# Encoder layer on one core: closer dense jobs beside attention, and partial results added before they are weighed

## The chip, the cores and the metric

The kernel runs on one core of a Trainium2 chip. The metric is the device time of one execution in microseconds (us), the median of several runs. The engines are TensorE (PE, matmuls, with PEld for its weight loads), VectorE (DVE), ScalarE (ACT), GpSimd (POOL) and SyncE (SP), which issues most of the transfers.

## The reference

One layer of an encoder, with a width of 1024, 2048 rows and one sequence:

```python
mod = c_act @ w_ada[l] + b_ada[l]
h = rmsnorm(x, g_norm1[l]) * (1.0 + sc1) + sh1
proj = h @ w_in[l]
q_sb, k_sb, v_sb, q_ca, k_ca, v_ca = jnp.split(proj, split_pts, axis=-1)
o_sb = stick_breaking_attention(...)        # 8 heads of 64, causal
o_ca = chunked_relpos_attention(...)        # 8 heads of 64, own chunk and 8 before it
mixed = jnp.concatenate([o_sb, o_ca], axis=-1)
x = x + gt1 * (mixed @ w_o[l])
h = rmsnorm(x, g_norm2[l]) * (1.0 + sc2) + sh2
x = x + gt2 * (jnp.square(jax.nn.relu(h @ w1[l])) @ w2[l])   # 1024 -> 4096 -> 1024
```

All of it is float32. The stick-breaking heads weigh a key by its own sigmoid and by the product of one minus the sigmoids of the keys between.

## The kernel before

Every float32 operand is split into a high part (rounded to the matmul's fp32r) and a low part (the rest), and a product takes three matmuls: high by high, high by low, low by high. ACT copies the high part, DVE (or POOL) subtracts it. Rows are worked on in four blocks of 512.

The stages follow each other: projections (0 to 413 us of the span), attention (413 to 1290), a seam, and the MLP (1330 to the end). PE, DVE, ACT and POOL run their instructions in the order in which the program issues them.

**Attention** is a list of units: one head `h`, one block of rows `g` and, for the stick-breaking heads, one block of keys. Each has four steps. In a step, PE computes scores (`z`), ACT and DVE turn them into weights (DVE's scan is `p`), PE transposes the weights of a unit eight steps older (`wt`), ACT and DVE split them (`wth`, `wtl`), and PE multiplies them with the values (`acc`). The softmax heads' names begin with `c`. Blocks of rows are taken in the order 2 and 3 together, 1, 0.

PE has time left in a step, which is filled with dense matmuls of 512 columns. They come from jobs that are run one after the other: the projections of the row blocks 1 and 0 (`fill_qkv`, banks `pf`), and the output projection of the blocks 2, 3 and 1 (`outproj`, banks `po`, eight banks of 24 matmuls). Each job is a generator: it yields a number for a matmul, a function for work that is put off, and the words "ahead" and "wait". `fill`, called once in a step, adds the step's share to a credit and takes matmuls from the job while the credit is at least one. At "wait", which each job yields once before its first matmul, it sets a rest from `RESTS`: for so many steps no dense matmul is taken. At "ahead", which a job yields near its end, the next job's `ahead` issues transfers: input tiles (`fx`) and one set of weights (`ow` or `fw`). The tiles come in groups of four from rotating pools, so a group's transfer has to wait until the tiles that it overwrites have been used.

When both heads of a pair are done, `finish` adds their halves on POOL, and some steps later `keep` splits the result (ACT copies `os`, POOL subtracts) and stores it. `values` in `fill_qkv` does the same split for the value projections, with ACT and DVE.

**The MLP** saves matmuls with sums and differences of operand blocks: a group takes seven products instead of eight. Five groups of its second matmul, class `Outer` with `i` in (7, 2, 5, 3, 4), run the products 1, 5, 6, 3, 7, 2, 4 in this order. A product has eight steps of six matmuls. For each step ACT and DVE make the operands (`opr`, `ol`), eight steps ahead, and DVE also makes sums of the right-hand operand (`r`, `half_sum`). At a product's end its two banks (`ps`, `ps_s`) go to the output blocks that they belong to: `weigh` on DVE multiplies a bank by the gate and adds it to an output tile `x`. In the groups 7 and 5, the blocks "22" and "12" each take two products and go into two output tiles per half. The output tiles are loaded with the residual by `load_x`.

Of the kernel before, what the change touches and what calls it, by code (L numbers as in the profile page):

```python
# [9 lines left out]
F32 = mybir.dt.float32  # L10
# [3 lines left out]
ALU = mybir.AluOpType  # L14
# [65 lines left out]
def encoder_kernel(ctx, tc, xT, c, g1, g2, w_in, w_rest, gqk, bias, w_o, w1, w2, w_ada, b_ada, out):  # L80
# [602 lines left out]
    if True:  # L683
# [36 lines left out]
        def finish(u):  # L720
            r = (u.h % 2) * HD
            q = HD - r
            if u.h % 2 == 0:
                pend["o", u.g] = op.tile([P, TB], F32, tag="o", name=f"o{u.nm}")
            o = pend["o", u.g]
            tmp = op.tile([P, TB], F32, tag="otmp", name=f"otmp{u.nm}")
            rows = slice(r, r + HD)
            act.copy(tmp[rows, :], u.acc[q : q + HD, :])
            act.copy(o[rows, :], u.acc[rows, :])

            def add():
                pool.tensor_tensor(o[rows, :], o[rows, :], tmp[rows, :], op=ALU.add)
                if u.h % 2:
                    wait(6 if u.g == 3 else 2, lambda: keep(u, o))

            soon.append(add)

        def wait(steps, job):
            soon.append(job if steps == 1 else lambda: wait(steps - 1, job))
# [203 lines left out]
            def weights(self, qi, kb):  # L943
                return self.ws[qi][:, (kb - qi) * P : (kb - qi + 1) * P]

        RESTS = {"wait": 4, "start": 0}
        resident = {}
        svs = []
        turn = [0]
# [1 line left out]
        class Filler:  # L951
# [17 lines left out]
            def ahead(self):  # L969

                if self.src:
                    self.fetch(KT // 2)
                self.load()

            def load(self):
# [13 lines left out]
        def fill_qkv(self, tb, ht, pieces):  # L989

            self.tiles = ht or []
            wide = [p for p in pieces if p in VALS]

            def narrow_load(piece, i):
                w = ring.tile([P, KT // 2, 2, CW], F32R, tag="r8", name=f"fw{tb}_{piece}_{i}")
                ldq.dma_start(w.bitcast(F32), scr_w[piece,][:, i * 4 : i * 4 + 4, :, :])
                return {i * 4 + k: w[:, k] for k in range(KT // 2)}

            def wide_load(piece, k, n):
                if n == 2:  # L1000
                    w = ring.tile([P, 2, 2, TB], F32R, tag="r8", name=f"fw{tb}_{piece}_{k}")
                else:
                    pl = (hx2, hxp, hxp)[turn[0] % 3]
                    w = pl.tile([P, 1, 2, TB], F32R, tag="hx", name=f"fv{tb}_{piece}_{k}")
                sp.dma_start(w.bitcast(F32), scr_wv[piece // 6,][:, k : k + n])
                return {k + i: w[:, i] for i in range(n)}

            def loads(piece):
                if piece not in wide:
                    return [lambda i=i: narrow_load(piece, i) for i in range(2)]  # L1010
                halves = [(0, 1), (1, 1), (2, 1), (3, 1), (4, 2), (6, 2)]
                if piece != wide[0]:
                    halves = [(0, 2), (2, 1), (3, 1), (4, 1), (5, 1), (6, 2)]
                return [lambda k=k, n=n: wide_load(piece, k, n) for k, n in halves]

            parts = [{} for _ in pieces]
            banks = [(n, j) for n, piece in enumerate(pieces) for j in range(4 if piece in wide else 2)]
            plan = {}
            for n, piece in enumerate(pieces[1:], 1):

                at, old = banks.index((n, 0)) - 1, pieces[n - 1]
                if piece not in wide:
                    times = [(at, 0), (at, 4 if old not in wide else 6 if old == wide[0] else 2)]
                elif old not in wide:
                    times = [(at - 3 + i, 2) for i in range(4)] + [(at, 0), (at, 4)]
                else:
                    times = [(at, 0), (at, 4), (at, 5), (at, 6), (at, 7), (at, 6)]
                for t, job in zip(times, loads(piece)):
                    plan.setdefault(t, []).append((n, job))

            self.loaders = loads(pieces[0])
            yield None if ht else lambda k: scr_h[:, k]
            ht = self.moving()
            for got in self.first():
                parts[0].update(got)
            yield "wait" if tb == 0 else "start"
            for at, (n, j) in enumerate(banks):
                piece, w = pieces[n], parts[n]
                last = at + 1 == len(banks) or not banks[at + 1][1]
                nm = f"f{tb}_{piece}_{j}"  # L1040
                ps = dense.tile([P, TB], F32, tag="ps", name=f"p{nm}")
                cl = slice(j * P, (j + 1) * P)
                for k in range(KT):
                    for m, job in plan.pop((at, k), ()):
                        parts[m].update(job())
                    if at + 1 == len(banks) and k in (0, 4):
                        yield "ahead"
                    for i, (a, b) in enumerate(((0, 0), (0, 1), (1, 0))):
                        flags = {"start": k == 0 and i == 0, "stop": k == KT - 1 and i == 2}
                        if piece in wide:  # L1050
                            pe.matmul(ps, ht[k][:, b, cl], w[k][:, a, :], **flags)
                        else:
                            pe.matmul(ps, w[k][:, a, cl], ht[k][:, b, :], **flags)
                        yield 1.0

                def keep():
                    if piece not in wide:
                        st = fp.tile([P, 2, TB], F32R, tag="st", name=f"st{nm}")
                        store_qk(piece // 2, 0, ps, st, piece % 2 * 2 + j, tb)
                    else:  # L1060
                        if j % 2 == 0:
                            svs[:] = [
                                fp.tile([P, NH // 2, 2, 2, HD], F32R, tag="st", name=f"sv{nm}_{hf}") for hf in range(2)
                            ]
                        for hf, sv in enumerate(svs):
                            half = ps[:, hf * CW : (hf + 1) * CW].rearrange("p (h d) -> p h d", d=HD)
                            split(sv[:, :, j % 2, 0, :], sv[:, :, j % 2, 1, :], half)
                            if j % 2:
                                sp.dma_start(
                                    scr_v[piece // 6, tb, hf][:, :, j - 1 : j + 1, :].rearrange("h p t e -> p h (t e)"),  # L1070
                                    sv.rearrange("p h t l d -> p h (t l d)").bitcast(F32),
                                )
                    if last:
                        have.add((piece, tb))

                yield keep

        def outproj(self, g):
# [11 lines left out]
            for n in range(KT):  # L1090
# [4 lines left out]
                    ws.append(load(n + 2))  # L1095
                if n + 1 < KT:
                    rx = load_residual(g, n + 1, xrp)
                else:
                    yield "ahead"
                    yield "ahead"  # L1100
                ps = dense.tile([P, TB], F32, tag="ps", name=f"po{g}_{n}")
                for k in range(KT):
                    for i, (l, m) in enumerate(((0, 0), (0, 1), (1, 0))):
                        pe.matmul(
                            ps, w[:, l, k, :], mx[k][:, m, :], start=k == 0 and i == 0, stop=k == KT - 1 and i == 2
                        )
                        yield 1.0
# [218 lines left out]
    PLAIN = (1, 6)  # L1326
    DOUBLE = (7, 2, 5, 3, 4)
    OUTER = (1, 5, 6, 3, 7, 2, 4)
    OUTER_NAME = {1: "11", 2: "12", 4: "22"}
    HOME = {1: 1, 2: 1, 5: 5, 3: 5, 6: 6, 7: 6, 4: 6}  # L1330
    HP = NP // 2
# [6 lines left out]
    if True:  # L1338
# [431 lines left out]
        class Outer(Step):  # L1770
# [50 lines left out]
            def end(self, n):  # L1821
                pr, ps = self.pr, Outer.banks[HOME[self.pr], n]
                if pr == 1:
                    Outer.banks[6, n] = bank(f"{self.nm}_s{n}", seeded)
                    act.copy(Outer.banks[6, n], ps)
                for b, done in {5: (("22", 0),), 6: (("12", 0),), 3: (("12", 1),), 7: (("22", 1),), 2: (("11", 1),), 4: (("21", 1),)}.get(pr, ()):
                    for x, mb, row, odd, last in Outer.outs[b, n]:
                        weigh(x, ps, row)
                        if done:
# [1 line left out]
                            later.add(2, lambda dst=dst, x=x: sp.dma_start(dst, x))  # L1831

            def load_x(self, b):
                home = kept if self.i in (5, 7) and b in ("22", "11") else temp
                for n in range(2):
                    Outer.outs[b, n] = []
                    for r, odd in {2: ((0, 1),), 3: ((0, 0),), 4: ((1, 1),), 7: ((1, 1), (1, 0)), 5: ((0, 0), (1, 0))}[self.i]:
# [23 lines left out]
        def outer(i, plan):  # L1861
# [7 lines left out]
                    at(begin + gap * g, lambda pr=pr, g=g: half_sum(i, pr, g))  # L1869
            for q in range(7):  # L1870
                at(f + HP * q - 12, steps[f + HP * q].load)
            for pr, b in ((5, "22"), (6, "12"), (2, "11"), (4, "21")):
                s = steps[f + HP * OUTER.index(pr)]
                at(f + HP * OUTER.index(pr) + (1 if b == "22" else -5), lambda s=s, b=b: s.load_x(b))
            return f

        class Mixed(Step):
# [218 lines left out]
```

## Time and profile before

| | |
|---|---|
| median of 3 runs | 2537.08 us (2535.84 to 2537.11) |
| profiled execution, its own time | 2536.57 us |
| its span | 2534.8 us, so 1.8 us lie outside |
| granted TensorE clock | 0.998 |
| busy PE / DVE / ACT / POOL | 2511.2 / 2032.4 / 1523.8 / 773.9 us |

The busy time of an engine is the sum of its instructions, and the end of a matmul is modelled. Each wait is named by the instruction that ended it: `PE z <- DVE p` is PE's scores waiting for DVE's scan.

### The profile page before, as it was taken

To read this page: it belongs to the slowest core of one execution; us is meant where nothing else is said; L and a number is where in the kernel's file an instruction comes from. 1 tells how busy PE (TensorE), PEld (TensorE's weight loads), DVE (VectorE), ACT (ScalarE), POOL (GpSimd) and SP (SyncE) were. 2 spreads that over 40 slices of the span, in tenths; PEclk is the share of its full clock that TensorE was granted. 3 is DMA by queue.
4 is the path that set the end of the run, shared out by engine and by line. 5 is a ranking of instruction groups with operands and counts; after the bars stand their busy time and mean duration, and the time that the engine had idled before them with its cause. 6 is when DMAs were issued, how large, how long until landed. Compare 5 with 4: busy or idle time off the path is not lost.

```text
span 2534.8 us, 39551 instructions
## 1 busy us (share of the span) xinstructions
PE 2511.2 (99%) x12388; PEld 2097.2 (83%) x12388; DVE 2032.4 (80%) x3577; ACT 1523.8 (60%) x2917; POOL 773.9 (31%) x1160
## 2 busy tenths in 40 slices
PE   9999999999999999999999999999999999999999
PEld 8888888888878888788888888888888888888787
DVE  7656776887789988999868777779877759799998
ACT  6334424668866687666755555567555546576665
POOL 4330154776766677777620000000000000010000
PEclk9999999999999999999999999999999999999999
DMA  9879968779977788766777889996998996888882
GB/s 356 325 300 361 354 272 293 225 244 289 297 246 250 236 245 268 257 196 212 228 284 260 298 278 321 328 351 207 315 323 270 314 365 260 321 248 286 299 282 84
DMA packets 300755, 706.29 MB, mean 279 GB/s; under 512 B 32256, under 2 KB 91648, under 8 KB 288896
## 3 DMA queue, kind: packets, MB, share of 16 engines
q1 hardware_dynamic: 294640, 690.65, 79.5%
q0 software_dynamic: 4608, 8.39, 1.9%
q10 hardware_dynamic: 1296, 4.72, 0.5%
q8 instruction: 98, 1.61, 0.3%
q14 instruction: 113, 0.93, 0.1%
HBM read 476.61 MB, written 227.02 MB: 278 GB/s over the span
## 4 chain that ended last, share of the span: by engine, by line
PE 48%; DVE 7%; ACT 1%; DMA 1%; issue 1%; SPq 0%; POOL 0%; DVEq 0%; ACTq 0%; POOLq 0%
PE ps L42 25%; PE ps_s L42 14%; PE po L42 3%; PE acc L42 2%; PE wt L42 2%; DVE opr L42 2%; PE z L42 1%; DVE ol L42 1%; DVE r L42 1%; DVE h L42 1%; DVE txo L42 0%; PE cz L42 0%; ACT cy L42 0%; DVE cy L42 0%; ACT h L42 0%
## 5 line engine op out<-in xcount | busy, mean ns | idle before, releaser
L42 PE MATMUL ps<-h,opw 128*128 128x512 f32 x1512 | 358.6, 390 | 0.0
L42 ACT CAST wth<-wt 128x512 fp32r<-128x512 f32 (+3 forms) x544 | 257.1, 484 | 167.8 <-PE wt L42 157.1
L42 POOL TENSOR_TENSOR b<-p 128x512 f32<-128x512 f32 (+1 forms) x320 | 291.9, 912 | 167.1 <-DVE p L42 103.8
L42 DVE TENSOR_TENSOR wtl<-wt,wth 128x512 fp32r<-128x512 f32 (+3 forms) x544 | 291.0, 547 | 60.8 <-ACT wth L42 58.1
L42 PEld LDWEIGHTS ps<-h,opw 128*128 128x128 f32 x1512 | 283.9, 188 | 58.7
L42 PE MATMUL pt<-w,ht 128*128 128x512 f32 x1248 | 288.2, 391 | 0.0
L42 PE MATMUL ps_s<-h,opw 128*128 128x512 f32 x1152 | 277.5, 390 | 0.7 <-DVE cp L42 0.3
L42 PEld LDWEIGHTS pt<-w,ht 128*128 128x128 f32 x1248 | 233.1, 188 | 47.6
L42 DVE TENSOR_TENSOR_SCAN p<-z,p,zero 128x512 f32<-128x512 f32 x192 | 245.5, 1280 | 21.2 <-ACT z L42 16.4
L42 PEld LDWEIGHTS ps_s<-h,opw 128*128 128x128 f32 x1152 | 215.9, 188 | 46.7 <-DVE cp L42 0.9
L42 ACT CAST opr<-r 128x512 fp32r<-128x512 f32 x280 | 174.3, 623 | 129.1 <-PE ps L42 72.1
L42 PE MATMUL ps<-opr,ol 128*128 128x512 f32 x960 | 222.0, 390 | 0.4 <-DVE opr L42 0.3
L42 PE MATMUL acc<-wth,v 128*128 128x512 f32 (+3 forms) x544 | 220.9, 410 | 0.1
L42 PEld LDWEIGHTS ps<-opr,ol 128*128 128x128 f32 x960 | 179.9, 188 | 40.1 <-DVE opr L42 1.9
L42 ACT ACTIVATE z<-z 128x512 f32<-128x512 f32 (+1 forms) x320 | 166.5, 521 | 55.4 <-PE z L42 50.7
L42 DVE TENSOR_TENSOR opr<-r,opr 128x512 fp32r<-128x512 f32 x280 | 184.4, 681 | 10.8 <-ACT opr L42 10.0
L42 PE MATMUL z<-k,q 128*128 128x512 f32 (+3 forms) x640 | 185.8, 372 | 6.2 <-DVE p L42 5.5
L42 PE MATMUL acc<-wtl,v 128*128 128x512 f32 (+3 forms) x544 | 185.8, 348 | 0.1
L42 POOL DMA_DIRECT2D scr_x<-txu x12 | 10.5, 878 | 546.8 <-ACT txu L42 546.8
L42 PE MATMUL ps<-oph,opv 128*128 128x512 f32 x768 | 175.2, 390 | 0.3 <-DVE txo L42 0.2
L42 PE MATMUL wt<-ident,b 128*128 128x128 f32 x1088 | 171.2, 273 | 0.2 <-DVE p L42 0.2
L42 PEld LDWEIGHTS ps<-oph,opv 128*128 128x128 f32 x768 | 144.1, 188 | 30.9 <-DVE txo L42 0.6
(223 smaller groups left out, 5052.3 us busy)
## 6 DMA issues: line engine op xcount, KB each, us to landing
r<-scr_hid SPq DMA_DIRECT2D x80, 512.0 KB, 6.6
q<-scr_q SPq DMA_DIRECT2D x128, 256.0 KB, 5.3
w<-in_w_dram SPq DMA_DIRECT2D x64, 512.0 KB, 5.8
k<-scr_k SPq DMA_DIRECT2D x240, 128.0 KB, 4.1
v<-scr_v SPq DMA_DIRECT2D x120, 256.0 KB, 4.3
wa<-in_w_ada_dram SPq DMA_DIRECT2D x48, 512.0 KB, 6.2
ow<-scr_wo SPq DMA_DIRECT2D x24, 1024.0 KB, 6.7
l<-scr_t SPq DMA_DIRECT2D x20, 1024.0 KB, 7.7
```

Source lines behind the costliest of these rows:

```text
L42: return lambda *x, **y: self.tc.keep_in_program_order(f(*x, **y))
```

## The change

It has five parts. The rest after "wait" goes from four steps to one; `ahead` fetches four tiles more at each call, and `outproj` yields its two "ahead" inside the last bank, at its first and its fifth step, and no longer before it. `keep` comes two steps later for the row blocks 0 to 2. In `values`, the two ACT copies are written ahead of the two DVE differences. In the groups 7 and 5 of the MLP, the first of the two products of "22" and "12" is copied by ACT into a tile `q`; when the second is there, DVE adds it to `q` and weighs the sum into the output tiles; the tiles of "22" and "12" are loaded later.

```diff
@@ finish
-                    wait(6 if u.g == 3 else 2, lambda: keep(u, o))
+                    wait(6 if u.g == 3 else 4, lambda: keep(u, o))
...
-        RESTS = {"wait": 4, "start": 0}
+        RESTS = {"wait": 1, "start": 0}
...
             def ahead(self):
                 if self.src:
-                    self.fetch(KT // 2)
+                    self.fetch(min(KT, len(self.tiles) + KT // 2))
                 self.load()
...
+                        part = [ps[:, hf * CW : (hf + 1) * CW].rearrange("p (h d) -> p h d", d=HD) for hf in range(2)]
                         for hf, sv in enumerate(svs):
-                            half = ps[:, hf * CW : (hf + 1) * CW].rearrange("p (h d) -> p h d", d=HD)
-                            split(sv[:, :, j % 2, 0, :], sv[:, :, j % 2, 1, :], half)
+                            act.copy(sv[:, :, j % 2, 0, :], part[hf])
+                        for hf, sv in enumerate(svs):
+                            dve.tensor_tensor(
+                                sv[:, :, j % 2, 1, :], part[hf], sv[:, :, j % 2, 0, :].bitcast(F32), op=ALU.subtract
+                            )
...
@@ outproj
                     rx = load_residual(g, n + 1, xrp)
-                else:
-                    yield "ahead"
-                    yield "ahead"
                 ps = dense.tile([P, TB], F32, tag="ps", name=f"po{g}_{n}")
                 for k in range(KT):
+                    if n + 1 == KT and k in (0, 4):
+                        yield "ahead"
...
+    TWICE = (5, 7)
...
                 for b, done in {5: (("22", 0),), 6: (("12", 0),), 3: (("12", 1),), 7: (("22", 1),), 2: (("11", 1),), 4: (("21", 1),)}.get(pr, ()):
+                    if self.i in TWICE and b[1] == "2":
+                        if not done:
+                            Outer.outs[b, n, "part"] = kept(f"q{self.nm}_{n}")
+                            act.copy(Outer.outs[b, n, "part"], ps)
+                            continue
+                        c = Outer.outs.pop((b, n, "part"))
+                        ps = column_sum(dve, c, ps, c, ALU.add)
                     for x, mb, row, odd, last in Outer.outs[b, n]:
                         weigh(x, ps, row)
...
-                home = kept if self.i in (5, 7) and b in ("22", "11") else temp
+                home = kept if self.i in TWICE and b in ("22", "21") else temp
...
-            for pr, b in ((5, "22"), (6, "12"), (2, "11"), (4, "21")):
+            for pr, b in ((7 if i in TWICE else 5, "22"), (3 if i in TWICE else 6, "12"), (2, "11"), (4, "21")):
                 s = steps[f + HP * OUTER.index(pr)]
-                at(f + HP * OUTER.index(pr) + (1 if b == "22" else -5), lambda s=s, b=b: s.load_x(b))
+                at(f + HP * OUTER.index(pr) + (1 if pr == 5 else -5), lambda s=s, b=b: s.load_x(b))
```

PE at the seam of the output projections of row blocks 2 and 3, before; the first row is the last matmul of the old job, `z` are scores (one row in each step), the last row is the first matmul of the new job:

```order
L42 MATMUL po_7_13007<-fx_7_10848,ow_7_12521 128x512 x3
...
L42 MATMUL z_2_0_3_0_13223<-k_2_0_3_13034,q_2_0_12721 128x512 x2
...
L42 MATMUL z_2_0_3_1_13249<-k_2_0_3_13034,q_2_0_12721 128x512 x2
...
L42 MATMUL z_2_0_3_2_13281<-k_2_0_3_13034,q_2_0_12721 128x512 x2
...
L42 MATMUL z_2_0_3_3_13308<-k_2_0_3_13034,q_2_0_12721 128x512 x2
...
L42 MATMUL z_3_0_0_0_13328<-k_3_0_0_13134,q_3_0_13131 128x512 x2
...
L42 MATMUL z_3_0_0_1_13351<-k_3_0_0_13134,q_3_0_13131 128x384 x2
L42 MATMUL po_0_13358<-fx_0_12995,ow_0_13003 128x512 x3
```

Six steps' scores stand between the two jobs. The same place in PE's order of the changed program:

```order
L42 MATMUL po_7_12930<-fx_7_10714,ow_7_12455 128x512
...
L42 MATMUL z_2_0_2_2_13192<-k_2_0_2_12947,q_2_0_12737 128x512 x2
...
L42 MATMUL acc_1_0_0_12828<-wth_1_0_3_0_13136,v_1_0_3_12886 128x512
L42 MATMUL acc_1_0_0_12828<-wtl_1_0_3_0_13137,v_1_0_3_12886 128x512
L42 MATMUL z_2_0_2_3_13216<-k_2_0_2_12947,q_2_0_12737 128x512 x2
L42 MATMUL po_0_13223<-fx_0_12931,ow_0_12939 128x512 x3
L42 MATMUL po_0_13223<-fx_1_12933,ow_0_12939 128x512 x3
```

Two steps' scores are left between them. The old job ends two steps earlier in attention's order, and the new job begins six steps earlier.

DVE in group 7 of the MLP at the end of product 3, before (`opr`, `ol` and `r` are operands of the products to come, `txo_12` the output tiles of block "12", and the rows named TENSOR_SCALAR are `weigh`):

```order
L42 TENSOR_TENSOR opr_7_3_24670<-r_7_1_24281,opr_7_3_24670 128x512
L42 TENSOR_SCALAR txo_12_01_24418<-ps_5_0_0_24378,mod,txo_12_01_24418 128x512
L42 TENSOR_SCALAR txo_12_00_24420<-ps_5_0_0_24378,mod,txo_12_00_24420 128x512
L42 TENSOR_SCALAR txo_12_11_24422<-ps_5_0_1_24382,mod,txo_12_11_24422 128x512
L42 TENSOR_SCALAR txo_12_10_24424<-ps_5_0_1_24382,mod,txo_12_10_24424 128x512
L42 TENSOR_TENSOR opr_7_4_24683<-r_7_2_24308,opr_7_4_24683 128x512
L42 TENSOR_TENSOR ol_7_4_24686<-l_7_0_24534,ol_7_4_24686 128x512
L42 TENSOR_TENSOR r_4_1_24689<-r_2_1_24322,r_6_1_24217 128x1024
L42 TENSOR_TENSOR opr_7_5_24703<-r_7_2_24308,opr_7_5_24703 128x512
```

The same place after the change, where `cq_6_7` is the kept copy of product 6:

```order
L42 TENSOR_TENSOR opr_7_3_24670<-r_7_1_24281,opr_7_3_24670 128x512
L42 TENSOR_TENSOR cq_6_7_0_24570<-ps_5_0_0_24378,cq_6_7_0_24570 128x512
L42 TENSOR_SCALAR txo_12_01_24504<-cq_6_7_0_24570,mod,txo_12_01_24504 128x512
L42 TENSOR_SCALAR txo_12_00_24506<-cq_6_7_0_24570,mod,txo_12_00_24506 128x512
L42 TENSOR_TENSOR cq_6_7_1_24572<-ps_5_0_1_24382,cq_6_7_1_24572 128x512
L42 TENSOR_SCALAR txo_12_11_24508<-cq_6_7_1_24572,mod,txo_12_11_24508 128x512
L42 TENSOR_SCALAR txo_12_10_24510<-cq_6_7_1_24572,mod,txo_12_10_24510 128x512
L42 TENSOR_TENSOR opr_7_4_24685<-r_7_2_24308,opr_7_4_24685 128x512
L42 TENSOR_TENSOR ol_7_4_24688<-l_7_0_24526,ol_7_4_24688 128x512
L42 TENSOR_TENSOR r_4_1_24691<-r_2_1_24322,r_6_1_24217 128x1024
L42 TENSOR_TENSOR opr_7_5_24705<-r_7_2_24308,opr_7_5_24705 128x512
```

Four weighings from a bank have become two adds and four weighings from the kept tile; at the end of product 6 the four that stood there are gone, and ACT has two copies instead.

## The prediction

> **What bounds the kernel now.** I read the page first, then the table of stretches, the waits of TensorE, and the timelines of the stretches in which it waits. The page names the busy engines:
>
> ```profile
> PE 2511.2 (99%) x12388; PEld 2097.2 (83%) x12388; DVE 2032.4 (80%) x3577; ACT 1523.8 (60%) x2917; POOL 773.9 (31%) x1160
> PE 48%; DVE 7%; ACT 1%; DMA 1%; issue 1%; SPq 0%; POOL 0%; DVEq 0%; ACTq 0%; POOLq 0%
> ```
>
> PE is busy for 99% of 2534.8 us. The change takes no matmul away, so what it can win is PE's waits. A share of 99% doesn't say how large these are. The page's ends of matmuls are modelled, so I count by starts. The columns below are the stretch, its length, and busy time with (count) of PE, PEld, DVE, ACT and POOL, then the clock, the DMA share and GB/s:
>
> ```profile
> 1394.10:1457.50 63.40, 63.40 (x281) 52.56 (x280) 46.95 (x75) 37.03 (x67) 0.00 (x0) 1.00 0.84 298
> 599.40:608.60 9.20, 8.04 (x54) 6.67 (x53) 7.80 (x32) 7.99 (x22) 6.60 (x7) 1.00 0.89 284
> 881.30:889.90 8.60, 6.27 (x42) 5.07 (x41) 7.19 (x25) 7.19 (x14) 4.59 (x6) 1.00 0.89 280
> 1042.90:1055.00 12.10, 10.28 (x59) 7.58 (x58) 10.42 (x12) 7.21 (x15) 10.21 (x14) 1.00 0.66 226
> 1189.10:1199.20 10.10, 8.88 (x51) 6.91 (x50) 9.75 (x12) 6.29 (x13) 7.59 (x13) 1.00 0.65 222
> ```
>
> The first row is a stretch without waits: 63.40 / 281 = 0.2256 us from one 512-column matmul to the next. The other four are the places where one dense job of the attention stage ends and the next begins. `RESTS["wait"]` keeps four attention steps there free of dense matmuls. PE is shown idle for 1.16 + 2.33 + 1.82 + 1.22 = 6.53 us in them. The third one in the timeline of PE (start, duration, what ran; in brackets the idle time ahead and its releaser):
>
> ```profile
> 1043.77 0.37 PE L42 MATMUL acc<-wth,v 128*128 128x256 f32 x1
> 1043.97 0.28 PE L42 MATMUL acc<-wtl,v 128*128 128x256 f32 x1
> 1044.98 0.72 PE L42 MATMUL z<-k,q 128*128 128x512 f32 x2 [0.73 <-DVE p L42]
> ...
> 1045.98 0.31 PE L42 MATMUL acc<-wth,v 128*128 128x128 f32 x1
> 1046.12 0.27 PE L42 MATMUL acc<-wtl,v 128*128 128x128 f32 x1
> 1047.42 0.73 PE L42 MATMUL z<-k,q 128*128 128x512 f32 x2 [1.02 <-DVE p L42]
> ...
> 1051.41 1.77 PE L42 MATMUL po<-fx,ow 128*128 128x512 f32 x7
> ```
>
> PE waits for the bank of the next scores, which DVE's scan `p` frees. Two of the three gaps here are named. By starts they are larger: the 256-column `acc` takes 0.20 (1043.77 to 1043.97), but 1.01 pass from 1043.97 to 1044.98, so 0.81 is lost where 0.73 is shown; the next gap is 1.30 less 0.14, so 1.16 where 1.02 is shown. The same subtraction over all 206 matmuls of the four rows gives 2.1 + 3.2 + 3.15 + 1.97 = 10.4 us. The truth lies between 6.5 and 10.4, and I take the count by starts. The Trainium skill bears on this choice (Perfetto Trace Analysis, Identifying the Most-Contended Engine): it says that busy time of matmuls is no good measure, because pipelined instructions look smaller in the trace. In this trace they look larger (that `acc` is shown at 0.37 where 0.20 pass), which hides idle time all the same; by busy time alone the term below would be 5.5, and the sum 3.9 us smaller.
>
> The other half of the change is in two of the MLP's outer groups of products, called blocks 7 and 5 here. Block 7 runs from 2101.60 to 2178.09 and block 5 from 2298.24 to 2377.82:
>
> ```profile
> 2101.60 21.92 PE L42 MATMUL ps<-opr,ol 128*128 128x512 f32 x96
> ...
> 2156.00 11.38 PE L42 MATMUL ps<-opr,ol 128*128 128x512 f32 x48
> ...
> 2178.09 1.29 PE L42 MATMUL ps<-oph,opv 128*128 128x512 f32 x5
> ```
>
> ```profile
> 2298.24 21.92 PE L42 MATMUL ps<-opr,ol 128*128 128x512 f32 x96
> 2320.00 11.04 PE L42 MATMUL ps_s<-opr,ol 128*128 128x512 f32 x48
> 2330.88 11.58 PE L42 MATMUL ps<-opr,ol 128*128 128x512 f32 x48
> 2342.30 5.83 PE L42 MATMUL ps_s<-opr,ol 128*128 128x512 f32 x25
> 2348.48 2.03 PE L42 MATMUL ps_s<-opr,ol 128*128 128x512 f32 x6 [0.36 <-DVE opr L42]
> ...
> 2377.82 1.52 PE L42 MATMUL ps<-opr,ol 128*128 128x512 f32 x6
> ```
>
> A product of 48 matmuls takes 10.88 us (2320.00 to 2330.88), seven take 76.16. Block 7 takes 76.49 and loses 0.3; block 5 takes 79.58 and loses 3.4, and its PE waits for DVE's `opr`. There DVE has no pause at all:
>
> ```profile
> 2344.70:2408.10 63.40, 62.24 (x268) 49.57 (x267) 63.40 (x96) 39.83 (x68) 0.00 (x0) 1.00 0.86 299
> ```
>
> **The change part by part.** *Dense jobs one step apart* (`RESTS` 4 to 1, `Filler.ahead`, the two "ahead" points). No instruction is added. The order shows the new gap as one or two steps without dense matmuls instead of four, with the next job's first bank three to six steps earlier. A lone step without dense work has no named wait anywhere between the four places, so I let 1.0 us stand in all, and win 10.4 - 1.0 = **9.4** (6.5 less that would be 5.5; ends 5.5 and 10.4). What goes earlier is missing later: by the order the last softmax phase carries 72 dense matmuls in 32 steps instead of 80, and the waits of the rest of attention sum so:
>
> ```profile
> PE z L42 <- DVE p L42: 3.0, 4, 1.0
> PE cz L42 <- DVE cols L42: 1.4, 2, 1.0
> PE cz L42 <- DVE wtl L42: 1.2, 1, 1.2
> ```
>
> (us in total, times, longest, from 594 to 1290). Nothing prices a slightly thinner step; from below it is nothing, from above three waits of the longest kind, 3 x 1.0. I take **+1.0**, a single one, since eight matmuls of 0.2256 are 1.8 us spread over 32 steps. The loads that go earlier:
>
> ```profile
> ow<-scr_wo SPq DMA_DIRECT2D x24, 1024.0 KB, 6.7
> ```
>
> A weight tile lands 6.7 us after its issue. The second "ahead" point stands at half of the last bank. From there to the first use of what it fetches lie 24 dense matmuls (5.4 us) and by the order some 60 rows of attention work, in all 18 us at the pace of the rows above. The load's issue waits for the tile that it overwrites, whose last use is that same half bank, so it does not sit at SP's head for long. I price this at nothing; uncovered it would be 6.7 us at a place.
>
> *Heads' split two steps later* (`wait(4)`). The same copy, subtraction and store, moved past two steps on ACT, POOL and SP. Before, it fell just ahead of the next head's result copies on ACT:
>
> ```profile
> 467.69 0.62 ACT L42 CAST os<-o 128x512 fp32r<-128x512 f32 x1 [0.46 <-POOL o L42]
> ...
> 469.19 0.58 ACT L42 COPY otmp<-acc 64x512 f32<-64x512 f32 x1
> 469.77 0.58 ACT L42 COPY o<-acc 64x512 f32<-64x512 f32 x1
> ```
>
> ```profile
> PE z L42 <- DVE p L42: 2.6, 7, 0.6
> ```
>
> The last row is of 430 to 600, and three of its waits follow such a cluster (one is 0.44 at 472.34). Taking 0.6 us of ACT out of the cluster can win 0 to 2.0; I take **-1.0**. If it meets another cluster it costs one such wait, +0.6. No queue waits for the store: the job that reads it comes much later.
>
> *Value banks.* Only the code's order changes; each engine's own order is as before: **0**.
>
> *`TWICE`.* In blocks 7 and 5, DVE weighed both parts of "22" and "12" into two outputs from the bank. Now ACT copies the first part, DVE adds the second to the copy and weighs the sum. The prices:
>
> ```profile
> L42 DVE SCALAR_TENSOR_TENSOR txo<-ps,mod,txo 128x512 f32<-128x512 f32 x4 | 2.7, 733 | 0.0
> L42 ACT COPY cs<-ps 128x512 f32<-128x512 f32 x3 | 1.7, 588 | 0.1
> ```
>
> ```profile
> 2145.34 2.72 DVE L42 SCALAR_TENSOR_TENSOR txo<-ps,mod,txo 128x512 f32<-128x512 f32 x4
> 2147.97 0.68 DVE L42 TENSOR_TENSOR opr<-r,opr 128x512 fp32r<-128x512 f32 x1
> 2148.57 0.68 DVE L42 TENSOR_TENSOR ol<-l,ol 128x512 fp32r<-128x512 f32 x1
> 2149.18 1.22 DVE L42 TENSOR_TENSOR r<-r,r 128x1024 f32<-128x1024 f32 x1
> 2150.31 1.29 DVE L42 TENSOR_TENSOR opr<-r,opr 128x512 fp32r<-128x512 f32 x2
> ...
> 2157.47 2.72 DVE L42 SCALAR_TENSOR_TENSOR cxo<-ps_s,mod,cxo 128x512 f32<-128x512 f32 x4
> ```
>
> Four weighings hold DVE for 2147.97 - 2145.34 = 2.63 us. They vanish from the ends of products 5 and 6 (two ACT copies of 0.59 there instead), and at the ends of 3 and 7 two adds join them: one add like `opr` steps by 0.60 (2147.97 to 2148.57) and the weighing behind it needs its result, an estimate of 0.07 more, so 2.63 + 2 x 0.67 = 4.0, or +1.35. Per block DVE does 2 x 2.63 - 2 x 1.35 = 2.6 us less, but later. Operands are made eight tiles ahead, four of them beyond the product's end, so a DVE that is early at product 3's end can't use the saved time. Product 7 begins at 2156.00 - 10.88 = 2145.12, and a step of six matmuls takes 1.36. Its fifth step's operands must be there at 2145.12 + 4 x 1.36 = 2150.56, and the sixth at 2151.92; the sixth's was done at about 2150.99. That is 0.93 to spare, and 1.35 is more: 0.4 lost in product 7, and the whole 1.35 again in product 2, ahead of which DVE began its group 1.47 late already (2157.47 against 2156.00) and 0.3 was lost. Block 7: 0.4 + 1.35, and the half-sums behind them on DVE still to fit in, so **+2.5** (1.0 to 4.0). Block 5 was behind throughout, so it first wins: the waits in products 3 and 7 go (about 1.5 of its 3.4), then product 2 loses as in block 7: **0** (-1.5 to +1).
>
> The sum: -9.4 + 1.0 - 1.0 + 0 + 2.5 + 0 = **-6.9 us**. The profiled run took 2536.57 (1.8 outside its span), 0.5 under the median of 2537.08. That makes 2529.7 of it, and 2530.2 of the median.
>
> **Rivals.** *The gain is spent again* (0.27). Attention is near DVE's limit in its last part, as the stretches at 1042.90 and 1189.10 show (10.42 of 12.10 and 9.75 of 10.10 busy). If the thinner steps cost 3.0 and the four places win only 5.5, or `TWICE` costs 5, the sum is -5.5 + 3.0 - 1.0 + 2.5 = -1.0, or -4.4: 2532.7 to 2536.1. The waits listed speak against it, being few and short away from the four places.
>
> *DVE was the limit of both blocks* (0.14). If the six operations fit the slack after all, both blocks run at PE's pace: -0.3 - 3.4 instead of +2.5, a sum of -13.1, or 2524.0. The Trainium skill's rule for results of matmuls favours it (VectorE: DVE Perf Modes, Rules for kernel authors): copy PSUM to SBUF first if many operations follow. The rows are for it in block 5, whose DVE is full, and against it in block 7, which lost 0.3.
>
> *Slower: loads not landed* (0.09). If the fetches that now go out at the last bank sit behind a blocked row of SP, the first bank of each of the four jobs waits for one landing: 4 x 6.7 - 6.9 = +19.9, or 2557.0; at two places +6.5, at one about 0. It decides when issue to first use falls under 6.7 us; 18 are there.
>
> *The change does not do what it says* (in the first rival): dense matmuls held back by credit rather than by the rest. The order shows them earlier, so I leave it there.
>
> **How the numbers follow.** The forecast has 0.50, the rivals 0.27, 0.14 and 0.09. A measurement can tell about 0.2%, 5.1 us, so the line is 2532.0. Faster: all of the second rival, and of the forecast the part beyond the line: its own ends (2526 to 2534) leave about 0.08 short, 0.14 + 0.42 and 0.05 of the first rival, 0.61. Slower than 2542.2: the loads at two or more places, and a `TWICE` that costs more than all is won, 0.09. Same: 0.30. The range takes in the second rival's end and the first rival, without the loads: 2524 to 2537.5.
>
> **What would show it.** In the four places TensorE's named waits go from 6.5 us to under 2. Block 7 becomes 1 to 4 us longer, with waits `<- DVE opr` in products 7 and 2; block 5 stays at 78 to 81. DVE's group after product 3 lasts about 4.0 instead of 2.6. Wrong would be waits of `po` on `fx` or `ow`, new waits `z <- DVE p` of over 3 us after 1200, or block 7 unchanged.

## The result and the profile after

The changed kernel takes 2540.91 us (median of 20 runs) where the kernel before takes 2536.64 beside it: a ratio of 1.0015, with a 95% interval of 1.0009 to 1.0021. Forecast were 2530.2, and a range of 2524.0 to 2537.5. So it is slower by some 4 us, less than the 0.2% that I had called the line, and outside the range.

The profiled execution has a span of 2539.0, against 2534.8. PE's line of the page after:

```profile
PE 2510.5 (99%) x12388; PEld 2096.1 (83%) x12388; DVE 2026.3 (80%) x3569; ACT 1527.4 (60%) x2925; POOL 774.3 (30%) x1160
```

DVE is busy 6 us less, as it was meant to be, and PE's work is the same; the 4 us are waits, and matmuls at half the clock behind two of them. Where they arise is seen by taking the start of the same matmul in both traces and subtracting (after less before, in us; negative is ahead):

| the matmul | before at | after, earlier or later |
|---|---|---|
| a projection that the change doesn't touch | 21.0 | -1.3 |
| first scores of the softmax heads of blocks 2 and 3 | 573.1 | -5.3 |
| last dense matmuls of attention, `po` of bank 4 | 1289.8 | -5.4 |
| `po` of bank 7, behind the seam's wait | 1306.9 | +0.4 |
| block 7 of the MLP begins | 2101.6 | +0.6 |
| the next outer block (`i` = 2) begins | 2222.1 | +3.5 |
| block 5 has ended | 2377.8 | +4.4 |

The first 1.3 are chance, since the programs are alike there; the granted clock from 15 to 22 us was 0.53 before and 1.00 after. Attention wins about 4, the seam takes nearly 6, and blocks 7 and 5 nearly 4.

**The four places** are covered, as forecast. Stretches of the trace after around them (columns as in the prediction):

```profile
595.00:605.00 10.00, 9.95 (x65) 8.40 (x64) 8.58 (x33) 8.85 (x24) 7.16 (x9) 1.00 1.04 347
872.00:881.00 9.00, 7.75 (x42) 6.29 (x41) 7.87 (x18) 6.35 (x11) 4.99 (x8) 1.00 0.97 269
1031.00:1041.00 10.00, 10.00 (x53) 7.99 (x52) 8.82 (x11) 7.32 (x14) 6.80 (x10) 1.00 0.83 263
1178.00:1188.00 10.00, 10.00 (x54) 8.20 (x52) 9.65 (x13) 6.91 (x14) 6.94 (x11) 1.00 0.83 252
```

PE is idle for 1.3 us in them instead of 6.5. But there are new waits of PE behind them. The waits from 605 to 698 of the trace after (in us: total, times, longest):

```profile
PE ct L42 <- DVE cols L42: 1.4, 1, 1.4
PE wt L42 <- DVE wtl L42: 1.2, 1, 1.2
PE cz L42 <- DVE wtl L42: 0.6, 1, 0.6
```

The trace before names a single one there, from 609 to 700:

```profile
PE wt L42 <- DVE cols L42: 0.4, 1, 0.4
```

From 1188 on there is another one. In the timeline of PE after, the first matmuls of the new job's second bank stand behind the norm's `prm`, and wait until DVE has emptied the first bank:

```profile
1198.85 1.05 PE L42 MATMUL prm<-ndgm,ones 128*128 128x128 f32 x8
...
1200.65 0.51 PE L42 MATMUL cz<-k,q 128*128 128x384 f32 x2
1202.54 1.90 PE L42 MATMUL po<-fx,ow 128*128 128x512 f32 x7 [1.38 <-DVE xr L42]
```

**The first 96 steps** lose their waits. From 430 to 600 the wait `z <- DVE p` was 2.6 us in seven waits; after it is

```profile
PE z L42 <- DVE p L42: 0.2, 1, 0.2
```

**The seam.** Where attention ends, the last three banks of `po` of row block 1 are left. PE's timeline, before and then after:

```profile
1289.79 11.12 PE L42 MATMUL po<-fx,ow 128*128 128x512 f32 x48
1301.33 10.90 PE L42 MATMUL po<-fx,ow 128*128 128x512 f32 x47 [0.41 <-DMA ow<-scr_wo]
```

```profile
1284.39 11.11 PE L42 MATMUL po<-fx,ow 128*128 128x512 f32 x48
1300.11 12.09 PE L42 MATMUL po<-fx,ow 128*128 128x512 f32 x45 [4.62 <-DMA ow<-scr_wo]
```

PE comes 5.4 us earlier and waits 4.6 for the weights. SP's issues say why, again before and then after (start, duration, what is issued):

```profile
1287.80 0.32 SPq L746 DMA_DIRECT2D scr_m<-os  x1
1288.22 2.15 SPq L42 DMA_DIRECT2D opm<-scr_m  x4
1290.47 0.39 SPq L42 DMA_DIRECT2D ow<-scr_wo  x1
```

```profile
1285.55 0.32 SPq L746 DMA_DIRECT2D scr_m<-os  x1
1285.97 2.52 SPq L42 DMA_DIRECT2D opm<-scr_m  x4
1288.58 0.77 SPq L42 DMA_DIRECT2D ow<-scr_wo  x1
```

The load of `ow` stands behind the store of a pair of heads of row block 0 and behind four loads of its results, and that store is one of those that now come two steps later. Of the 5.4 us only 1.9 reach the load, and from its issue to PE's start pass 11.5 us instead of 10.9 (1288.58 to 1300.11, and 1290.47 to 1301.33). SP itself waits for the data of the stores, from 1270 to 1305, before and then after:

```profile
SPq L746 <- POOL os L42: 8.9, 2, 6.7
```

```profile
SPq L746 <- POOL os L42: 15.9, 2, 8.9
```

The wait on `ow` is 4.2 longer, but the seam takes 5.8 (-5.4 to +0.4). The other 1.6 are the matmuls behind the wait. The first eight, before and then after:

```profile
1301.33 2.06 PE L42 MATMUL po<-fx,ow 128*128 128x512 f32 x8 [0.41 <-DMA ow<-scr_wo]
```

```profile
1300.11 3.49 PE L42 MATMUL po<-fx,ow 128*128 128x512 f32 x8 [4.62 <-DMA ow<-scr_wo]
```

After, they step by 0.427 us instead of 0.227. Two stretches of the trace after show the granted clock at 0.50 (third number from the right), this one and one in product 2 of block 5:

```profile
1300.40:1303.80 3.40, 3.40 (x9) 2.63 (x8) 0.75 (x1) 0.00 (x0) 0.00 (x0) 0.50 1.01 386
2365.40:2368.80 3.40, 3.38 (x8) 2.16 (x8) 3.40 (x7) 0.73 (x2) 0.00 (x0) 0.50 0.89 261
```

**Blocks 7 and 5.** PE's timeline of block 7 after, products 7 and 2:

```profile
2145.67 7.19 PE L42 MATMUL ps_s<-opr,ol 128*128 128x512 f32 x31
2153.02 4.15 PE L42 MATMUL ps_s<-opr,ol 128*128 128x512 f32 x17 [0.17 <-DVE opr L42]
2157.01 5.83 PE L42 MATMUL ps<-opr,ol 128*128 128x512 f32 x25
2164.28 2.03 PE L42 MATMUL ps<-opr,ol 128*128 128x512 f32 x6 [1.45 <-DVE opr L42]
2166.62 4.15 PE L42 MATMUL ps<-opr,ol 128*128 128x512 f32 x17 [0.31 <-DVE opr L42]
```

### The profile page after: what moved, and what is told of

It is laid out like the page before. It is cut to its first block, busy times and chain, and to the rows that moved or that the text cites. A ratio compares the mean times of both kernels' runs of the same rounds, so it can differ in the third digit from the quotient of the medians.

```text
span 2539.0 us, 39554 instructions
## 1 busy us (share of the span) xinstructions
PE 2510.5 (99%) x12388; PEld 2096.1 (83%) x12388; DVE 2026.3 (80%) x3569; ACT 1527.4 (60%) x2925; POOL 774.3 (30%) x1160
## 4 chain that ended last, share of the span: by engine, by line
PE 87%; DVE 5%; DMA 3%; ACT 3%; issue 2%; POOL 0%; SPq 0%; DVEq 0%; ACTq 0%; POOLq 0%
PE ps L42 25%; PE ps_s L42 14%; PE pt L42 11%; PE acc L42 7%; PE wt L42 7%; PE pf L42 6%; PE z L42 5%; PE po L42 5%; PE pq L42 3%; PE pso L42 2%; PE cz L42 1%; DVE opr L42 1%; PE ct L42 1%; PE px L42 1%; DVE ol L42 0%
## 5 line engine op out<-in xcount | busy, mean ns | idle before, releaser
L42 PE MATMUL po<-fx,ow 128*128 128x512 f32 x576 | 164.3, 397 | 6.0 <-DMA ow<-scr_wo 4.6
```

Of the source, the lines that this page charges most:

```text
L42: return lambda *x, **y: self.tc.keep_in_program_order(f(*x, **y))
```

## The experiments

All are compared with the kernel before, run on the same chip beside them. The waits of PE below are counted by starts, as in the prediction: the time from one matmul to the next less the pace of its size, summed over attention's steps. "Places" are the 38 steps around the four ends of jobs. Three numbers hold some 1.6 us of half clock besides waits, each from one stretch of 3.4 us in that trace: the places of e1 (from 883 us) and e3 (from 1049), and the other steps of e8 (from 706). "Jobs" are the dense jobs one step apart; the changed kernel, e4, e5, e6 and e9 also have the new order of the value banks, the other runs don't.

| kernel | us | ratio, 95% interval | first 96 steps | places | other steps | wait on `ow` at the seam |
|---|---|---|---|---|---|---|
| before | 2536.64 to 2537.13 | | 9.0 | 11.1 | 17.9 | 0.4 |
| changed | 2540.91 | 1.0015 (1.0009 to 1.0021) | 4.8 | 3.6 | 25.1 | 4.6 |
| e1, jobs only | 2536.68 | 0.9998 (0.9989 to 1.0007) | 8.9 | 5.6 | 23.9 | 0.8 |
| e2, split only | 2536.75 | 0.9999 (0.9990 to 1.0008) | 6.6 | 11.3 | 17.8 | 3.7 |
| e3, added first only | 2539.94 | 1.0012 (1.0003 to 1.0021) | 9.6 | 12.0 | 18.5 | 1.2 |
| e4, changed without added first | 2536.49 | 0.9997 (0.9988 to 1.0006) | 4.5 | 3.7 | 25.2 | 5.0 |
| e5, changed, block 0 split early | 2536.67 | 0.9999 (0.9991 to 1.0008) | 4.5 | 3.9 | 24.5 | 0.8 |
| e6, changed, `ow` ahead of `opm` | 2537.84 | 1.0005 (0.9996 to 1.0014) | 5.6 | 3.7 | 25.6 | 1.3 |
| e7, split of 1 and 2, `ow` ahead | 2535.01 | 0.9993 (0.9984 to 1.0002) | 6.7 | 11.4 | 18.3 | none |
| e8, rest of 7 | 2540.18 | 1.0014 (1.0004 to 1.0023) | 8.8 | 10.9 | 22.6 | 2.0 |
| e9, jobs, value banks, split of 1 and 2 | 2533.61 | 0.9981 (0.9972 to 0.9990) | 4.5 | 3.9 | 25.1 | 0.3 |
| e10, split of 1 and 2 only | 2535.46 | 0.9994 (0.9985 to 1.0003) | 6.6 | 11.4 | 17.8 | 1.4 |

**The jobs alone** (e1): the kernel before with

```diff
-        RESTS = {"wait": 4, "start": 0}
+        RESTS = {"wait": 1, "start": 0}
-                    self.fetch(KT // 2)
+                    self.fetch(min(KT, len(self.tiles) + KT // 2))
 # and the two "ahead" of outproj inside its last bank
```

> The kernel before with the dense jobs one step apart alone (the rest of 1, the fetch of eight tiles, the two points inside the last bank). Theory (the waits move): the four places lose about 6.8 us of waiting, but steps 112 to 160, 272 to 320 and 416 on get about as much, as in the changed kernel; 2536.6, within 2 us, and at the seam no wait on ow above 2 us. Rival (the four places pay, as predicted, and something else in the change ate it): 8 us are won, 2528 to 2530.

Measured: nothing is won. The places wait 5.5 us less, or some 7 without the half clock, and the other steps 6.0 more. The named waits of its attention from 594 on are, among smaller ones,

```profile
PE ct L42 <- DVE cols L42: 2.1, 4, 1.4
PE wt L42 <- DVE p L42: 1.5, 4, 0.7
PE po L42 <- DVE xr L42: 1.4, 1, 1.4
```

**The split alone** (e2): `wait(6 if u.g == 3 else 2, ...)` becomes `wait(6 if u.g == 3 else 4, ...)`.

> The kernel before with the heads' split two steps later alone. Theory (SP's queue at the seam): attention is about 4 us shorter, all of it ahead of 556 us, but the last stores come two steps later, the load of ow that stands behind them on SP lands late and PE waits for it for 3 to 5 us: 2535.5 to 2538. Rival (the seam's wait has to do with the jobs): 4 us are won, 2532.5, with a wait on ow under 1 us.

Measured: 2.4 us fewer waits in the first 96 steps, not 4, and a wait of 3.7 on `ow`, which was 0.4, so all of it is lost again. The theory of SP's queue holds without any of the jobs' change.

**Added first alone** (e3): the five places of `TWICE` put into the kernel before.

> The kernel before with the partial results added first alone, in the outer blocks 7 and 5. Theory: block 7 is 2.6 us longer, block 5 1.1 us, with PE waiting for opr in product 2 of both: 2540.3. Rival (the slack differs from run to run and the change is nil): 2536.6.

Measured: 2539.94. By starts block 7 is 2.8 us longer, and block 5 0.3 shorter; I had expected 1.1 longer, as the changed kernel shows (1.0). That 1.0 holds 1.2 us of half clock, in the stretch from 2365.4 above; without it both traces agree. A row of DVE's timeline of e3 in product 3, and the group of six at that product's end:

```profile
2137.92 0.69 DVE L42 TENSOR_TENSOR opr<-r,opr 128x512 fp32r<-128x512 f32 x1 [1.15 <-ACT opr L42]
...
2147.63 0.68 DVE L42 TENSOR_TENSOR cq<-ps,cq 128x512 f32<-128x512 f32 x1
2148.35 1.42 DVE L42 SCALAR_TENSOR_TENSOR txo<-cq,mod,txo 128x512 f32<-128x512 f32 x2
2149.68 0.68 DVE L42 TENSOR_TENSOR cq<-ps,cq 128x512 f32<-128x512 f32 x1
2150.40 1.42 DVE L42 SCALAR_TENSOR_TENSOR txo<-cq,mod,txo 128x512 f32<-128x512 f32 x2
2151.73 0.69 DVE L42 TENSOR_TENSOR opr<-r,opr 128x512 fp32r<-128x512 f32 x1
```

From 2147.63 to 2151.73 are 4.10 us, where four weighings took 2.63. Ahead of it DVE stands idle for ACT's casts (1.15 us in the first row), so the time that it saves there is lost.

**The changed kernel without it** (e4):

> The changed kernel without the partial results added first: the outer blocks as before. Theory: attention 5 us shorter, the seam's wait of 4.6 us on ow stays, and nothing is lost in the blocks 7 and 5: 2537. Rival (the blocks are nil): 2540.9.

Measured: 2536.49, as the theory has it. The wait of 5.0 on `ow` is still there.

**Row block 0 split early again** (e5): in the changed kernel,

```diff
-                    wait(6 if u.g == 3 else 4, lambda: keep(u, o))
+                    wait((2, 4, 4, 6)[u.g], lambda: keep(u, o))
```

> The changed kernel with the heads' split of row block 0 at two steps again (blocks 1 and 2 stay at four). Theory (the store of the last pair but one heads SP's queue at the seam, and two steps' delay of it is the delay of the load of ow behind it): SP issues that store some 4 us earlier, PE's wait on ow falls from 4.6 to about 1 us, 2537.2. Rival (the load is late because the transfers of that moment share the bandwidth): the load goes out earlier and lands when it did, the wait stays over 3 us, 2540.5.

Measured: the store goes out 3.2 us earlier, the load of `ow` 3.6, and PE waits 0.8. SP and PE at the seam in e5:

```profile
1282.36 0.32 SPq L746 DMA_DIRECT2D scr_m<-os  x1
1282.78 2.16 SPq L42 DMA_DIRECT2D opm<-scr_m  x4
1285.03 0.47 SPq L42 DMA_DIRECT2D ow<-scr_wo  x1
```

```profile
1284.34 11.13 PE L42 MATMUL po<-fx,ow 128*128 128x512 f32 x48
1296.23 11.16 PE L42 MATMUL po<-fx,ow 128*128 128x512 f32 x48 [0.76 <-DMA ow<-scr_wo]
```

Attention ends as early as in the changed kernel, and now PE keeps it. From the load's issue to PE's start pass 11.2 us, between the 10.9 of before and the 11.5 of the changed kernel: the load is hardly quicker, its issue moved.

**The load ahead of the others** (e6): in the changed kernel, at the seam,

```diff
-        steps[0].fetch(0, KT // 2)
         row()
+        steps[0].fetch(0, KT // 2)
         row()
```

> The changed kernel with the load of ow ahead of the four loads of opm on SP at the seam (one call moved down a line). Theory of the queue: the load goes out 2.6 us earlier and without 2 MB ahead of it, the wait on ow goes away (0 to 1 us), 2536.5. Rival (bandwidth): the wait stays above 3 us. A third: the loads of opm are late instead, by as much.

Measured: in between. With the four loads behind it the load is there 6.5 us after its issue (6.3 in e7), where it took 10.7 before and 11.4 in the changed kernel. So it is in time, but the next one, of the last bank, is now behind the four loads and comes 1.3 us late:

```profile
1303.62 5.72 PE L42 MATMUL po<-fx,ow 128*128 128x512 f32 x24 [1.33 <-DMA ow<-scr_wo]
```

This is the expectation's third case in part: the wait goes to what stands behind.

**Split of blocks 1 and 2, load ahead** (e7): e5's and e6's lines in the kernel before.

> The kernel before with two things: the heads' split at four steps for the blocks 1 and 2 only, and the load of ow ahead of the loads of opm. Theory: the 2 to 3 us that the later split wins in attention come out at the end, 2533.5 to 2534.5, with no wait on ow. Rival (what attention wins at the seam is always lost there): 2536.8.

Measured: 2535.01, with no wait on `ow`, half a microsecond above the expected span; the interval reaches to no change.

**A rest of seven** (e8): `RESTS = {"wait": 7, ...}` in the kernel before.

> The kernel before with a rest of seven steps instead of four. Theory (the idle time of attention is set by DVE's share of it and only moves: what the dense matmuls don't cover at one place they cover at the next): the four places wait 4 to 8 us more and the rest of attention as much less, 2537 to 2539. Rival (each step without dense matmuls costs its own wait): 10.4 / 4 x 3 = 7.8 us or more, 2544.5 and up.

Measured: 2540.18, between the two, and neither mechanism: the places wait as long as before (10.9), and the other steps 4.7 more, or some 3 without the half clock. So the idle time of attention isn't a fixed amount that only moves; my theory fell in this form.

**What is left when both losses are taken out** (e9): the changed kernel without `TWICE`, and with e5's line. The order of the value banks is in it too, which the expectation leaves out.

> The changed kernel without the partial results added first, and with the heads' split of row block 0 at two steps: what is left are the dense jobs one step apart and the later split of the blocks 1 and 2. Theory: attention ends 4 to 5 us earlier, the seam's wait on ow is under 1 us, the outer blocks are as before: 2531.5 to 2532.5. Rival (a fixed end: what is won ahead is lost behind): 2536.5.

Measured: 2533.61, a ratio of 0.9981 (0.9972 to 0.9990), 1 to 2 us above the expected. Its wait on `ow` is 0.3. It is the only one of these kernels whose interval lies below 1.

**The split of blocks 1 and 2 alone** (e10): e5's line in the kernel before.

> The kernel before with the heads' split of the blocks 1 and 2 at four steps, nothing else. Theory: the split alone takes 2.4 us of waits out of the first 96 steps, and nothing is lost at the seam: 2534.0 to 2535.0. Rival (the jobs carry the gain, the split only with them): 2536.5.

Measured: 2535.46. The waits go from 9.0 to 6.6 as expected; the wait on `ow` is 1.4, so a part is lost. e9 ran beside it and is 1.85 lower.

Of what e9 has more, the jobs are not the part that acts in the first 96 steps (4.5 against 6.6): PE takes the same matmuls there in the same order in both, and e1 wins nothing there. The value banks act. ACT's rows of one value bank, in e10 and then in e9:

```profile
483.37 0.38 ACT L42 CAST svf<-pf 128x256 fp32r<-128x256 f32 x1
485.05 0.37 ACT L42 CAST svf<-pf 128x256 fp32r<-128x256 f32 x1 [1.30 <-DVE svf L42]
```

```profile
483.48 0.66 ACT L42 CAST svf<-pf 128x256 fp32r<-128x256 f32 x2
```

With the old order ACT's second copy waits until DVE has taken the first difference. Over the whole program these waits of ACT are 13.5 us before, and nothing after:

```profile
L42 ACT CAST svf<-pf 128x256 fp32r<-128x256 f32 x24 | 9.0, 374 | 13.5 <-DVE svf L42 13.4
```

```profile
L42 ACT CAST svf<-pf 128x256 fp32r<-128x256 f32 x24 | 7.8, 384 | 0.0
```

They are 13 to 16 us in e1, e2, e7 and e10, and zero in e4, e5, e6 and e9.

**One of the two blocks at a time** (e11 and e12): e3 with `b == "12"` or `b == "22"` in place of `b[1] == "2"`, and the loads of the other block as before.

> The kernel before with the partial results of block "12" alone added first (the six operations stand at the end of product 3; the end of product 7 has its four weighings as before). Theory: in group 7 product 7 loses 0.5 us and product 2 about 0.5 of DVE's delay that is left; group 5 gains about 1: 2536 to 2537.5. Rival (the loss is the copies' on ACT): half of 2.6, 2538.

> The same for block "22" alone (the six operations stand at the end of product 7). Theory: nothing in product 7 and 1.3 to 2.0 us more in product 2 of group 7, none in group 5, which was behind there before: 2538 to 2539. Rival (the loss is the copies' on ACT): half of 2.6, 2538, but spread over both products.

Measured: 2536.96 and 2538.35, with ratios of 1.0002 (0.9993 to 1.0011) and 1.0004 (0.9995 to 1.0013), so the times decide nothing. The starts do: with "12", block 7 loses 0.4 in product 7 and 1.0 in product 2; with "22", nothing in product 7 and 1.4 in product 2. The sum of both is 2.8, what e3 lost. Block 5 is 1.2 shorter with "12" and 0.3 shorter with "22". ACT's copies stand at the end of 6 with "12" and of 5 with "22", and nothing is lost there.

## Why the prediction was wrong

Two steps of it failed: the price of the thinner steps, put at 1.0, and the price of the later store, put at nothing.

**The dense jobs** (-9.4, and +1.0 for thinner steps): the first is mis-sized a little, the second is the step that failed, and the largest miss. The places win 7.5, but the other steps pay 7.2, not 1.0. This is the first rival, the gain that is spent again, at more than twice its price of 3.0. I had bounded this from above by three waits of the longest kind, because the rest of attention had few named waits. That was a count of what happens with the work lying as it did, and no bound on what happens when it lies elsewhere. By the starts, 3.4 of the 7.2 lie in steps 116 to 160 and 3.6 in the last forty. From step 416 on there are 13 dense matmuls fewer (73 against 86), and the `po <- DVE xr` of 1.4 is a bank that the norm's job takes at that moment. In steps 116 to 160 there is one fewer (113 against 114), so thinner steps can't be the reason. Which steps they fall into has changed, and that this is the cause is only argued. e1, with the jobs alone, pays about half of the 3.4 there. No run separates the rest, so its cause stays open, and e8 shows that a longer rest costs as well.

**The split** (-1.0): the direction held and the size was too small. It wins 2.4 alone. With all the parts it is 4.2, of which the other 1.8 go with the value banks.

**"No queue waits for the store"** is the step that turned the sign. It was true of the row blocks that I looked at, whose results are read much later. It was false of row block 0, whose stores are the last rows on SP before the loads of the seam. The price of the seam is 5.8, of which 4.2 are the longer wait and 1.6 the half clock behind it. The sign of being wrong, waits of `po` on `ow`, came here. My rival on the slower side had the right mechanism, a fetch behind a blocked row of SP, at the wrong place: I had put it at the four ends of jobs, where no wait on `fx` or `ow` is seen. e2, e5 and e9 show the cause from both sides: the later store alone brings the wait, and with the store back at its place the wait is 0.8 or less.

**`TWICE`** (+2.5 for block 7, 0 for block 5): right for block 7, by its own steps: the group lasts 4.10 where I had 4.0, product 7 loses 0.5 (0.4), product 2 2.4. Block 5 came out at -0.3 in e3, by the forecast's own steps: products 3 and 7 win 1.7 and product 2 loses 1.5. The +1.0 of the changed kernel is the 1.2 us of half clock in its product 2. The rival that DVE was the limit of both blocks fell. The Trainium skill's rule to copy PSUM to SBUF first if many operations follow (VectorE: DVE Perf Modes, Rules for kernel authors) found no support here: a weighing from the kept tile steps by 0.665 us (2148.35 to 2149.68 for two) and one from the bank by 0.658 (2.63 for four). What the copy saves is the number of operations; two uses of each part were too few to pay at the point where DVE is late.

**Value banks** (0): this term was mis-sized too. I had reasoned that each engine's own order stays as it was. It does, but the order between the engines was a wait: ACT's second copy behind DVE's first difference, 13.5 us in all. Without it the first 96 steps wait some 2 us less (e9 against e10). No run has this part alone, so what it does behind step 96 is open.

The sum as measured: -1.3 by chance, -2.4 for the split, -1.8 for the value banks, -0.3 for the jobs, +5.8 at the seam, +2.9 and +1.0 for the blocks, and +0.3 in small differences, is +4.2, the difference of the spans. The jobs' -0.3 takes in whatever split and value banks do behind step 96.

## What to carry to other kernels

A change that leaves every engine's own order alone can still remove waits, if it changes what is written before what. When a store is put off, look for the last time that it is put off: at the end of a stage the queue behind it holds the next stage's loads, and a gain of the whole stage can end in that one wait. Idle time at a place where two engines are nearly balanced is worth what is left after the work that fills it is missed elsewhere; a bound for that is a run, not a count of waits that are there now. Work that is put together at the end of a product can cost the path even where it is less in sum, if the operands of the next product are made by the same engine.

## What the runs showed of the hardware

Executions of the same program repeat each other's waits in attention to about 1 us (the first 96 steps 8.8 to 9.6 in before, e1, e3 and e8; the other steps 17.8 to 18.5 in before, e2, e3, e7 and e10). So two profiles place a shift of 2 us, which the intervals of the times, about 4.5 us wide, don't. A load of 1 MB with 2 MB ahead of it on its queue was there 10.7 to 11.4 us after its issue at the seam (before, e5, changed), and 6.5 and 6.3 with the 2 MB behind it (e6, e7); the median of its kind is 6.7.

The granted clock was 0.5 for 3.4 us behind the seam's waits of 3.7 and 4.6 (e2, changed) and for 6.8 us behind that of 5.0 (e4). It stayed at 1.0 there behind waits of 0.8 and 2.0 (e5, e8). Shorter waits had it in some traces: of the eight blocks 7 and 5 in the changed kernel, e3, e5 and e6, all with a wait of about 1.4 us in product 2, three show such a stretch (block 5 of the changed kernel, block 7 of e5, block 5 of e6), at 1.0 to 1.2 us each. So in this kernel a wait of PE costs more than its own length at times, and not in every execution.
